# Accumulations of a seven-product block multiplication in PSUM tiles of their own, and accumulating DRAM transfers in another order and at another rate

## The chip, the cores and the metric

The kernel runs on one core of one Trainium2 chip. The metric is the device time of one execution in microseconds (us). Three runs of the kernel before gave 2103.21, 2102.78 and 2099.25 us; the median is 2102.78 us.

## The reference

Two transformer blocks follow each other on 512 tokens of width 1024, all in float32. Block 1 mixes a chunked gated delta rule (4 heads) with a differential attention (4 heads) and adds the result to its input. Block 2 puts 16 meta tokens ahead (528 tokens) and has a half-weighted feed-forward block, a hybrid mixer (retention and a sparse attention), and a second half-weighted feed-forward block. Only the feed-forward part matters here:

```python
def swiglu(u, w_gate, w_up, w_down):
    return (jax.nn.silu(u @ w_gate) * (u @ w_up)) @ w_down

h = h + 0.5 * swiglu(rmsnorm_2(h, ffn1_norm[l]), ffn1_w_gate[l], ffn1_w_up[l], ffn1_w_down[l])
h = h + hybrid_mixer(rmsnorm_2(h, mix_norm[l]), ...)
h = h + 0.5 * swiglu(rmsnorm_2(h, ffn2_norm[l]), ffn2_w_gate[l], ffn2_w_up[l], ffn2_w_down[l])
```

The feed-forward width is 2816, so that there are 22 column tiles `f` of 128 for the gate and 22 for the up weights.

## The kernel before

Activations lie transposed in SBUF (features on the 128 partitions, tokens along the free dimension). Every float32 product is made of three fp32r matmuls: a weight is split into a high part `whi` (ScalarE cast, line 238) and a rest `wlo` (VectorE subtraction, line 239), the activations likewise, and `whi*xhi + whi*xlo + wlo*xhi` is accumulated in PSUM.

One list of jobs (`jobs`) holds all weight loads of the program in the order of their use. `prefetch` issues them on SP's queue as buffers come free, `_conv` splits them (line 238 and 239, up to five split pieces ahead of the matmuls), and `w()` hands a piece to the matmuls.

**The feed-forward block (`ffn`).** The first three column tiles (`PLAIN = 3`) are multiplied plainly. The other 19 go through `pairs`, which treats gate and up weights of one `f` as a 2 x 2 block matrix (gate or up, lower or upper half of the 1024 inputs) and the tokens as two halves of 264 (256 in the second feed-forward block), and forms the four block products with seven multiplications in place of eight. Each multiplication is a `part` of 12 matmuls (4 input tiles, 3 terms each). For one `f` the parts on TensorE stand in this order, where `px`, `py` and `pz` are accumulators in PSUM:

1. `px` with the lower gate weights and the tokens `b11` (line 1053, in `begin`); ScalarE then copies it to `c1` (line 1055).
2. `py` with the token sums `t(0)` (line 1070); ScalarE then copies it to `c5` (line 1071).
3. the last part of the `f` before, into that `f`'s `px` (`end`, line 1059).
4. `px` further with `t(1)` (line 1074); ScalarE copies it to `c2` (line 1075).
5. `pz` with `b21` (line 1076); VectorE adds `c1` to it (line 1077).
6. `py` further with `b22` (line 1078); VectorE adds `c2` to it (line 1079).
7. `px` further with `t(2)` (line 1082); VectorE adds `c5` to it (line 1083).

`px` and `py` are the two halves, each one bank, of one PSUM tile `pm` of 128 x 2 x 512 (two buffers, line 1051); `pz` is a tile `sc` of its own (two buffers). The tiles `st` and `so` (one buffer of 128 x 512 each) serve the mixer. Waits between engines are put in by the tile framework, which also arranges the instructions of each engine; the first matmul of each part is kept in program order (line 1045).

`pairs` runs four times: for `f` 3 to 10 and 11 to 21 of each feed-forward block, 38 `f` in all, each time with the eight down projections of that half behind it.

**The weight sums (`sum_weights`).** Four of the seven products take sums of weight blocks. They are formed in DRAM by GpSimd's queue: plain transfers DRAM to DRAM, and transfers that accumulate (`accum_op`, line 226 to 228). The 19 column tiles are taken in ten chunks of two (the last of one). A chunk goes through six steps, eight transfers of 512 KB in all, of which each step needs the one before. The steps of different chunks are interleaved in waves: in a wave the first chunk does its step 0, the chunk before it step 1, and so on. The generator yields after each transfer and is moved on by `_conv`, once for every `bgn` splits: `bgn` is 1 for the first feed-forward block's sums (started ahead of block 1) and 3 for the second's (started ahead of the mixer). GpSimd's queue has little else: four `affine_select` of 128 x 512 (line 581) and three memsets in block 1's delta rule, four memsets in the mixer, two multiplications at the end. `pairs` reads the sums back through SP's queue as 256 KB quarters (`fraw<-wsffn`).

Of the kernel before, what the change touches and what calls it, by code (L numbers as in the profile page):

```python
# [168 lines left out]
class Net:  # L169
# [5 lines left out]
    def jobs(self, jobs):  # L175
        self.joblist = jobs
        self.j_dma = self.j_conv = self.k_conv = self.j_use = self.n_conv = self.n_use = 0
        self.p_dma = self.p_done = self.f_dma = self.f_done = 0
        self.raws, self.convd, self.wsums = {}, {}, {}
        self.bg, self.bgn = iter(()), 1  # L180
        self.kept = 0
        self.fpool = self.kslot = None
# [23 lines left out]
    def sum_weights(self, n):  # L206


        nc, a = self.nc, self.a
        nf = 22 - PLAIN  # L210
        out = self.wsums[n] = [self.dram.tile([min(2, nf - i), 4, 128, 4, 128], F32, name=f"ws{n}{i}")
                               for i in range(0, nf, 2)]
        rows = lambda x: x.rearrange("n p k c -> p n k c")

        def src(i, x):
            f = PLAIN + 2 * i
            o = 4 if x in "GU" else 0
            return a[n + ("_gate" if x in "gG" else "_up")][f:f + out[i].shape[0], :, o:o + 4, :]

        steps = (((0, "u"), (2, "g")), ((0, "U"), (2, "u")), ((1, 0),), ((1, "g"),), ((3, 1),), ((3, "G"),))  # L220
        for wave in range(len(out) + len(steps) - 1):
            for j, step in enumerate(steps):
                i = wave - j
                if 0 <= i < len(out):
                    for d, x in step:
                        y = out[i][:, x] if isinstance(x, int) else src(i, x)
                        kw = {"accum_op": OP.add} if j in (1, 3, 5) else {}
                        nc.gpsimd.dma_start(rows(out[i][:, d]), rows(y), **kw)
                        yield
# [734 lines left out]
    def ffn(self, t0, done, split=KB, half_done=None):  # L964
# [11 lines left out]
        h = n // 2  # L976
        parts = [(0, h), (h, h)] if n > 512 else [(0, n)]
        self.open_psum()
        with tc.tile_pool(name="ff", bufs=1) as pool:
# [46 lines left out]
            def gated(f, u):  # L1026
                A.copy(ahi[:, f, 0:n], u)
                V.tensor_sub(alo[:, f, 0:n], u, ahi[:, f, 0:n].bitcast(F32))

            def temp(x):  # L1030
                return pool.tile([128, n], F32, name=x, tag=x, bufs=2)
# [6 lines left out]
            def part(p, x, first=False, last=False):  # L1038

                whi, wlo = self.w()  # L1040
                for k in range(4):
                    for i, (y, z) in enumerate(((whi, 0), (whi, 1), (wlo, 0))):
                        ins = P.matmul(p, y[k], x(k)[z], start=first and k == i == 0, stop=last and k == 3 and i == 2,  # L1043
                                       skip_group_check=True)
                        if k == i == 0:
                            tc.keep_in_program_order(ins)

            def pairs(f0, f1):

                def begin():  # L1050
                    pm = self.pmain()
                    px, py = pm[:, 0, 0:h], pm[:, 1, 0:h]
                    part(px, b11, first=True)
                    c1 = pool.tile([128, h], F32, name="c1", tag="c1", bufs=2)
                    A.copy(c1, px)  # L1055
                    return px, py, c1

                def end(f, px, u, g):
                    part(px, t(3), last=True)
                    V.scalar_tensor_tensor(u[:, 0:h], px, -1.0, g[:, 0:h], op0=OP.mult, op1=OP.mult)  # L1060
                    gated(f % 11, u)

                left = None
                nxt = begin()
                for f in range(f0, f1):
                    px, py, c1 = nxt
                    pz = self.psc()[:, 0:h]
                    c2, c5 = (pool.tile([128, h], F32, name=x, tag=x, bufs=2) for x in ("c2", "c5"))
                    g, u = temp("g"), temp("u")
                    part(py, t(0), first=True)  # L1070
                    A.copy(c5, py)
                    if left:
                        end(*left)
                    part(px, t(1))
                    A.copy(c2, px)
                    part(pz, b21, first=True, last=True)
                    V.tensor_add(g[:, 0:h], pz, c1)
                    part(py, b22, last=True)
                    V.tensor_add(g[:, h:n], py, c2)
                    V.tensor_mul(g, g, r)  # L1080
                    A.activation(g, g, AF.Silu)
                    part(px, t(2))
                    V.tensor_add(u[:, h:n], px, c5)
                    V.scalar_tensor_tensor(u[:, h:n], u[:, h:n], -1.0, g[:, h:n], op0=OP.mult, op1=OP.mult)
                    left = f, px, u, g
                    if f + 1 < f1:
                        nxt = begin()
                end(*left)

            made = None  # L1090
            for half in range(2):
                for f in range(11 * half, 11 * half + 11):
                    if f >= PLAIN:
                        if f == PLAIN:
                            sides.drain(made)
                        pairs(f, 11 * half + 11)
                        break
                    hi, lo = self.w()
                    p = psum()
                    product(p, hi, lo, xs, 0, KB, True, True)  # L1100
                    if f == 0:
                        self.rstd([self.psc() for _ in range(2 if n > 512 else 1)], t0)
                        V.tensor_scalar(rh, r, 0.5, None, op0=OP.mult)
                        made = sides.add(sums())
                    g, u = temp("g"), temp("u")
                    V.tensor_mul(g, p, r)
                    A.activation(g, g, AF.Silu)
                    hi, lo = self.w()
                    p = psum()
                    product(p, hi, lo, xs, 0, KB, True, True)  # L1110
                    V.tensor_mul(u, p, g)
                    gated(f, u)
# [569 lines left out]
@with_exitstack  # L1682
def kernel(ctx: ExitStack, tc: tile.TileContext, a, out):
    net = Net(ctx, tc, a)
    net.jobs(jobs(a))
    net.setup()
    net.bg = net.sum_weights("ffn1")
    next(net.bg)
    net.block1()
    net.ffn(0, lambda m, x: net.prep(m, 2))  # L1690
    net.bg, net.bgn = net.sum_weights("ffn2"), 3
    next(net.bg)
    net.mixer()
    net.final(out)
# [17 lines left out]
```

## Time and profile before

| what | value |
|---|---|
| median of 3 runs (lowest to highest) | 2102.78 us (2099.25 to 2103.21) |
| the profiled execution: its own time | 2107.55 us |
| span of the profiled execution, first to last instruction | 2105.7 us |
| TensorE busy | 1939.5 us (92%) |
| VectorE busy, ScalarE busy | 1288.8 us (61%), 906.9 us (43%) |
| mean granted TensorE clock over the span | 0.970 of full speed |

Busy times of matmuls overlap one another and their ends are modelled, so that a share near 100% does not say that TensorE is at its peak; the starts of successive matmuls do. Idle time is put down to what released the engine. Block 1 fills about the first 460 us, the first feed-forward block lasts to about 860 us, the mixer to about 1715 us, and the second feed-forward block to the end.

### The profile page before, as it was taken

Reading aid. Unit: us, or ns where it says so; the run is one execution under the profiler, and the core shown is the slowest. Engines: PE = TensorE matmul, PEld = TensorE weight load, DVE = VectorE, ACT = ScalarE, POOL = GpSimd, SP = SyncE. Lnnn points to the kernel's source line nnn. Section 1 sums busy time; section 2 is a strip of 40 time slices with the busy share of each in tenths; the row PEclk is TensorE's granted clock in tenths of the full one; section 3 lists DMA queues with packets and bytes.
Section 4 is the critical chain, followed back from the end, with each engine's and each line's share of the span. In section 5 each row is a group of like instructions: output and inputs, shape, how many; then the busy total and the mean of one; then the engine's idle time right before and its main releaser. Section 6 shows DMA issues by size and latency. Waiting matters only on the chain. (4 is left out here: it accounts for less than half of the span.)

```text
span 2105.7 us, 31678 instructions
## 1 busy us (share of the span) xinstructions
PE 1939.5 (92%) x12138; PEld 1708.1 (81%) x12138; DVE 1288.8 (61%) x2590; ACT 906.9 (43%) x1774; POOL 153.9 (7%) x179
## 2 busy tenths in 40 slices
PE   6957668999899889999999999999999998898898
PEld 3845446888899889988989898888888888888887
DVE  4744534766655665699855454677754575646664
ACT  4523334554533553444343434344443364524553
POOL 4323443200000000000000000000000000000000
PEclk9987778999999999999999999999999999999999
DMA  9999999733434433321212121211122234434423
GB/s 296 292 231 253 264 278 257 187 131 112 152 110 120 151 117 91 120 76 66 98 68 96 66 90 61 100 61 70 61 74 97 100 129 137 148 98 150 153 87 95
DMA packets 119607, 281.36 MB, mean 134 GB/s; under 512 B 16192, under 2 KB 18720, under 8 KB 119392
## 3 DMA queue, kind: packets, MB, share of 16 engines
q1 hardware_dynamic: 86816, 198.60, 28.9%
q0 software_dynamic: 31552, 79.70, 16.2%
q8 instruction: 95, 1.56, 0.3%
q10 hardware_dynamic: 1088, 1.05, 0.1%
q14 instruction: 56, 0.46, 0.1%
HBM read 276.63 MB, written 82.36 MB: 170 GB/s over the span
## 5 line engine op out<-in xcount | busy, mean ns | idle before, releaser
L238 ACT CAST whi<-wraw 128x512 fp32r<-128x512 f32 (+1 forms) x476 | 277.1, 584 | 609.6 <-PE pm L304 473.0
L303 PE MATMUL pm<-xhi,whi 128*128 128x264 f32 (+3 forms) x1448 | 503.9, 348 | 15.4 <-DVE xc L910 14.3
L304 PE MATMUL pm<-xlo,whi 128*128 128x264 f32 (+3 forms) x1448 | 495.9, 342 | 0.0
L305 PE MATMUL pm<-xhi,wlo 128*128 128x264 f32 (+3 forms) x1448 | 494.4, 341 | 0.0
L239 DVE TENSOR_TENSOR wlo<-wraw,whi 128x512 fp32r<-128x512 f32 (+1 forms) x476 | 305.1, 641 | 206.6 <-ACT whi L238 197.6
L303 PEld LDWEIGHTS pm<-xhi,whi 128*128 128x128 f32 (+1 forms) x1448 | 276.5, 191 | 50.1 <-DVE xc L910 14.8
L305 PEld LDWEIGHTS pm<-xhi,wlo 128*128 128x128 f32 (+1 forms) x1448 | 276.0, 191 | 31.2 <-issue 2.8
L304 PEld LDWEIGHTS pm<-xlo,whi 128*128 128x128 f32 (+1 forms) x1448 | 276.4, 191 | 29.0 <-issue 2.5
L239 DVE TENSOR_TENSOR wlo<-fraw,whi 128x512 fp32r<-128x512 f32 x266 | 183.6, 690 | 127.6 <-ACT whi L238 109.3
L238 ACT CAST whi<-fraw 128x512 fp32r<-128x512 f32 x266 | 164.5, 618 | 206.8 <-issue 65.7
L1043 PE MATMUL pm<-thi,whi 128*128 128x264 f32 (+1 forms) x608 | 181.0, 298 | 56.4 <-ACT c L1055 33.9
L1043 PEld LDWEIGHTS pm<-thi,whi 128*128 128x128 f32 x608 | 115.2, 189 | 73.5 <-ACT c L1055 41.5
L1043 PE MATMUL pm<-thi,wlo 128*128 128x264 f32 (+1 forms) x608 | 172.2, 283 | 0.0
L1043 PE MATMUL pm<-tlo,whi 128*128 128x264 f32 (+1 forms) x608 | 172.1, 283 | 0.0
L303 PE MATMUL pm<-ahi,whi 128*128 128x264 f32 (+1 forms) x506 | 160.1, 316 | 0.0
L305 PE MATMUL pm<-ahi,wlo 128*128 128x264 f32 (+1 forms) x506 | 159.9, 316 | 0.0
L304 PE MATMUL pm<-alo,whi 128*128 128x264 f32 (+1 forms) x506 | 159.3, 315 | 0.0
L1043 PEld LDWEIGHTS pm<-tlo,whi 128*128 128x128 f32 x608 | 115.5, 190 | 0.0
L1043 PEld LDWEIGHTS pm<-thi,wlo 128*128 128x128 f32 x608 | 115.2, 189 | 0.0
L305 PEld LDWEIGHTS pm<-ahi,wlo 128*128 128x128 f32 x506 | 95.1, 188 | 6.1
L304 PEld LDWEIGHTS pm<-alo,whi 128*128 128x128 f32 x506 | 95.2, 188 | 5.7
L303 PEld LDWEIGHTS pm<-ahi,whi 128*128 128x128 f32 x506 | 95.2, 188 | 5.8
(456 smaller groups left out, 3532.7 us busy)
## 6 DMA issues: line engine op xcount, KB each, us to landing
wraw<-in_w_in SPq DMA_DIRECT2D x124, 512.0 KB, 3.3
fraw<-wsffn SPq DMA_DIRECT2D x152, 256.0 KB, 2.6
wsffn<-in_ffn_up POOLq DMA_DIRECT2D x54, 512.0 KB, 18.2
wsffn<-in_ffn_gate POOLq DMA_DIRECT2D x54, 512.0 KB, 17.3
fraw<-in_ffn_gate SPq DMA_DIRECT2D x76, 256.0 KB, 2.7
wsffn<-wsffn POOLq DMA_DIRECT2D x36, 512.0 KB, 17.6
wraw<-in_ffn_down SPq DMA_DIRECT2D x32, 384.0 KB, 3.0
wraw<-in_ffn_down SPq DMA_DIRECT2D x32, 320.0 KB, 2.9
```

What stands on the lines that cost most here:

```text
L238: self.nc.scalar.copy(hi, x)
L239: self.nc.vector.tensor_sub(lo, x, hi.bitcast(F32))
L303: mm(ps, whi, xhi, start=start, stop=False, **kw)
L304: mm(ps, whi, xlo, start=False, stop=False, **kw)
L305: mm(ps, wlo, xhi, start=False, stop=stop, **kw)
L1043: ins = P.matmul(p, y[k], x(k)[z], start=first and k == i == 0, stop=last and k == 3 and i == 2, skip_group_check=True)
```

## The change

Two edits. In `pairs`, `px` keeps the first half of the `pm` tile, and `py` gets a tile of its own, `st` for even and `so` for odd `f`. In `sum_weights`, the waves become groups of three chunks, each step done for the three chunks in turn; and the generator is moved on at every second split during block 1 and at every third from the first feed-forward block on.

```diff
@@ sum_weights @@
         steps = (((0, "u"), (2, "g")), ((0, "U"), (2, "u")), ((1, 0),), ((1, "g"),), ((3, 1),), ((3, "G"),))
-        for wave in range(len(out) + len(steps) - 1):
+        for i0 in range(0, len(out), 3):
             for j, step in enumerate(steps):
-                i = wave - j
-                if 0 <= i < len(out):
+                for i in range(i0, min(i0 + 3, len(out))):
                     for d, x in step:
                         y = out[i][:, x] if isinstance(x, int) else src(i, x)
                         kw = {"accum_op": OP.add} if j in (1, 3, 5) else {}
@@ pairs @@
                 def begin():
-                    pm = self.pmain()
-                    px, py = pm[:, 0, 0:h], pm[:, 1, 0:h]
+                    px = self.pmain()[:, 0, 0:h]
                     part(px, b11, first=True)
                     c1 = pool.tile([128, h], F32, name="c1", tag="c1", bufs=2)
                     A.copy(c1, px)
-                    return px, py, c1
+                    return px, c1
@@ pairs, loop over f @@
-                    px, py, c1 = nxt
+                    px, c1 = nxt
+                    py = (self.pst, self.pso)[f % 2]()[:, 0:h]
                     pz = self.psc()[:, 0:h]
@@ tile_two_blocks_kernel @@
-    net.bg = net.sum_weights("ffn1")
+    net.bg, net.bgn = net.sum_weights("ffn1"), 2
     next(net.bg)
     net.block1()
+    net.bgn = 3
     net.ffn(0, lambda m, x: net.prep(m, 2))
-    net.bg, net.bgn = net.sum_weights("ffn2"), 3
+    net.bg = net.sum_weights("ffn2")
     next(net.bg)
```

What moves on TensorE, at the first matmuls of part 2 of the second `f` of a `pairs` call (the three rows ahead are the end of part 1; `thi`, `tlo` are the token sums, and the brackets name the engine whose semaphore the row waits for). Before:

```order
L1043 MATMUL pm<-xhi,whi 128x264
L1043 MATMUL pm<-xlo,whi 128x264
L1043 MATMUL pm<-xhi,wlo 128x264
L1043 MATMUL pm<-thi,whi 128x264 [waits Activation_49]
L1043 MATMUL pm<-tlo,whi 128x264
L1043 MATMUL pm<-thi,wlo 128x264
```

With the change:

```order
L1042 MATMUL pm<-xhi,whi 128x264
L1042 MATMUL pm<-xlo,whi 128x264
L1042 MATMUL pm<-xhi,wlo 128x264
L1042 MATMUL st<-thi,whi 128x264
L1042 MATMUL st<-tlo,whi 128x264
L1042 MATMUL st<-thi,wlo 128x264 [waits DVE_49]
```

The wait for ScalarE at the first matmul of part 2 is gone; a wait for VectorE stands at the third, the first that needs the converted `wlo` piece. The parts themselves follow each other as before.

The same at the first matmul of part 7 of that `f` (ahead of it the end of part 6). Before:

```order
L1043 MATMUL pm<-xlo,whi 128x264
L1043 MATMUL pm<-xhi,wlo 128x264
L1043 MATMUL pm<-thi,whi 128x264 [waits DVE_49]
L1043 MATMUL pm<-tlo,whi 128x264
L1043 MATMUL pm<-thi,wlo 128x264
```

With the change:

```order
L1042 MATMUL st<-xlo,whi 128x264
L1042 MATMUL st<-xhi,wlo 128x264
L1042 MATMUL pm<-thi,whi 128x264 [waits Activation_49]
L1042 MATMUL pm<-tlo,whi 128x264
L1042 MATMUL pm<-thi,wlo 128x264 [waits DVE_49]
```

The first matmul waited for VectorE, which reads `py`; it now waits for ScalarE's copy `c2` of `px`, two parts back.

On GpSimd's queue, chunks of the first feed-forward block in block 1 (`wsffn` with a number is a chunk; the brackets name the transfer queue's semaphores, eight used in turn, whose earlier transfer the row waits for). Before:

```order
L228 DMA wsffn_100<-in_ffn_up 128x2x512 [waits DMASW0_49]
L228 DMA wsffn_100<-in_ffn_gate 128x2x512 [waits DMASW1_49]
L228 DMA wsffn_99<-in_ffn_up 128x2x512 [waits DMASW2_49]
L228 DMA wsffn_99<-in_ffn_up 128x2x512 [waits DMASW3_49]
L228 DMA wsffn_98<-wsffn_98 128x2x512 [waits DMASW4_49]
L228 DMA wsffn_97<-in_ffn_gate 128x2x512 [waits DMASW5_49]
L228 DMA wsffn_96<-wsffn_96 128x2x512 [waits DMASW6_49]
L228 DMA wsffn_95<-in_ffn_gate 128x2x512 [waits DMASW7_49]
```

With the change:

```order
L227 DMA wsffn_97<-in_ffn_gate 128x2x512 [waits DMASW7_49,DMASW4_49]
L227 DMA wsffn_98<-in_ffn_gate 128x2x512 [waits DMASW5_49]
L227 DMA wsffn_99<-in_ffn_gate 128x2x512 [waits DMASW6_49,DMASW1_49]
L227 DMA wsffn_97<-wsffn_97 128x2x512 [waits DMASW7_49]
L227 DMA wsffn_98<-wsffn_98 128x2x512 [waits DMASW3_49,DMASW0_49]
L227 DMA wsffn_99<-wsffn_99 128x2x512 [waits DMASW1_49]
L227 DMA wsffn_97<-in_ffn_gate 128x2x512 [waits DMASW2_49]
L227 DMA wsffn_98<-in_ffn_gate 128x2x512 [waits DMASW3_49]
L227 DMA wsffn_99<-in_ffn_gate 128x2x512 [waits DMASW4_49]
```

Before, each row waits for the transfer eight places back. With the change these rows wait for the one three places back; of the 24 transfers of a group nine do so, the other fifteen wait for one four to six places back or for none. In both programs 51 transfers stand ahead of the first `affine_select`, 4 between it and the second, and all 160 (the second feed-forward block's too) ahead of the mixer's memsets. SP's queue has the same order in both, and TensorE, ScalarE and VectorE have the same order in block 1.

## Rows read from the trace of the kernel before

**Rows 1.** The page: TensorE's busy time, then tenths in 40 slices.

```profile
PE 1939.5 (92%) x12138; PEld 1708.1 (81%) x12138; DVE 1288.8 (61%) x2590; ACT 906.9 (43%) x1774; POOL 153.9 (7%) x179
...
PE   6957668999899889999999999999999998898898
...
PEclk9987778999999999999999999999999999999999
DMA  9999999733434433321212121211122234434423
```

**Rows 2.** Stretches: us; engines' busy us (instructions); clock, DMA share, GB/s.

```profile
200.00:250.00 50.00, 31.30 (x117) 22.84 (x117) 20.02 (x77) 14.04 (x30) 21.16 (x24) 0.67 1.05 259
550.00:600.00 50.00, 45.68 (x362) 44.17 (x362) 32.95 (x59) 24.88 (x49) 0.00 (x0) 1.00 0.49 147
600.00:650.00 50.00, 50.00 (x415) 50.00 (x414) 20.69 (x39) 12.64 (x26) 0.00 (x0) 1.00 0.31 89
```

**Rows 3.** TensorE's waits in the pairs: us in total, times, longest us.

```profile
PE pm L1043 <- ACT c L1055: 33.9, 37, 1.2
...
PE pm L1043 <- DVE g L1079: 17.7, 34, 0.5
...
PE pm L1043 <- ACT c L1071: 3.5, 4, 0.9
```

**Rows 4.** Timeline of TensorE, first feed-forward block: start us, us, instruction, [idle before <-releaser].

```profile
500.30 0.28 PE L1043 MATMUL pm<-xhi,wlo 128*128 128x264 f32 x1
501.49 0.39 PE L1043 MATMUL pm<-thi,whi 128*128 128x264 f32 x1 [0.91 <-ACT c L1055]
501.72 0.28 PE L1043 MATMUL pm<-tlo,whi 128*128 128x264 f32 x1
...
505.68 0.29 PE L1043 MATMUL sc<-xhi,whi 128*128 128x264 f32 x1
...
507.13 0.28 PE L1043 MATMUL pm<-xhi,whi 128*128 128x264 f32 x1
...
508.46 0.28 PE L1043 MATMUL pm<-xhi,wlo 128*128 128x264 f32 x1
509.27 0.39 PE L1043 MATMUL pm<-thi,whi 128*128 128x264 f32 x1 [0.53 <-DVE g L1079]
```

**Rows 5.** Timeline of TensorE, second feed-forward block.

```profile
1753.62 0.28 PE L1043 MATMUL pm<-xhi,wlo 128*128 128x256 f32 x1
1754.42 0.39 PE L1043 MATMUL pm<-thi,whi 128*128 128x256 f32 x1 [0.52 <-DVE g L1079]
...
1757.28 0.28 PE L1043 MATMUL pm<-xhi,wlo 128*128 128x256 f32 x1
1758.46 0.39 PE L1043 MATMUL pm<-thi,whi 128*128 128x256 f32 x1 [0.91 <-ACT c L1055]
```

**Rows 6.** Timeline of GpSimd: the sums ahead of the first affine_select.

```profile
1.27 0.89 POOL L228 DMA_DIRECT2D wsffn<-in_ffn_up  x1 [0.82 <-POOLq L1703]
...
118.31 1.16 POOL L228 DMA_DIRECT2D wsffn<-in_ffn_up  x1 [3.71 <-DMA wsffn<-in_ffn_up]
129.80 0.64 POOL L581 TENSOR_SCALAR_AFFINE_SELECT te<-te 128x512 f32<-128x512 f32 x1 [10.32 <-DVE te L580]
```

**Rows 7.** Line 228 (the sums), whole run: durations ns, first and last start; landing.

```profile
L228 POOL DMA_DIRECT2D wsffn<-in_ffn_gate x60: 562/1128/1643, 2.1 to 403.2; - x60
...
DMA to landing us min/median/max: 4.5/17.7/32.4
```

**Rows 8.** DMA, first 400 us: queue, packets, MB, share; weight loads' us to landing.

```profile
q0 software_dynamic: 31084, 78.68, 83.7%
...
wraw<-in_w_in SPq DMA_DIRECT2D x32, 512.0 KB, 8.4
```

**Rows 9.** DMA in the mixer, 900 to 1100 us: the same loads.

```profile
wraw<-in_w_in SPq DMA_DIRECT2D x23, 512.0 KB, 3.2
```

**Rows 10.** Waits in the first 400 us: ScalarE's split for the weight loads.

```profile
ACT whi L238 <- DMA wraw<-in_w_in: 77.2, 10, 27.3
```

## The prediction

> **What bounds the kernel now.** I read the page first, then the stretches of 50 us, then TensorE's own waits and its timeline, and last the transfers and GpSimd. On the page [rows 1] TensorE is busy for 92% of the span and ten tenths full almost everywhere outside two places: the first seven slices (block 1), where its clock is also granted at less than full speed and the DMA engines are full, and the stretches at 8 tenths around slices 10 to 16 and 34 to 39, which are the `pairs` of the two feed-forward blocks. The stretches [rows 2] tell the two places apart. From 200 to 250 us (block 1) TensorE is busy for 31 of 50 us at a mean clock of 0.67, and the DMA share is 1.05. From 550 to 600 us (`pairs`) it runs at full clock, has 45.7 us busy with 362 matmuls, and the transfers take half of the DMA engines; in the down projections from 600 to 650 us, where nothing is waited for, it starts 415 matmuls of the same width. So the pairs lose time at full clock and the cause is not the DMA.
>
> TensorE's waits [rows 3] name it: 33.9 us for ScalarE's copy `c1`, 17.7 us for VectorE's sum at line 1079 and 3.5 us for the copy `c5`. The timeline [rows 4] shows where. Within a stream, a part of 12 matmuls takes 505.68 to 507.13, 1.45 us, so 0.121 us from start to start. At the start of part 2 the next matmul comes 1.19 us after the last of part 1 (500.30 to 501.49), and the one behind it 0.23 us later; at part 7 it comes 0.81 us after part 6 (508.46 to 509.27). Part 2 writes `py` and the copy it waits for reads `px`; part 7 writes `px` and the sum it waits for reads `py`. They share nothing but the tile.
>
> **Part one, `py` in its own tile.** As the order shows, both waits lose their engine. What stands in their place is older: part 2 now needs only the `st` or `so` buffer of two `f` ago, and part 7 the copy `c2`, which ScalarE starts two parts (2.9 us) earlier. So I take the whole gap. In the first feed-forward block the stall at part 2 costs 1.19 - 0.12 + 0.23 - 0.12 = 1.18 us, that at part 7 0.81 - 0.12 + 0.11 = 0.80 us. The first `f` of each of the four calls has no part 3 between, so that part 4 waits for `c5` as part 2 for `c1`: four stalls in [rows 3], with the same 1.18 us. The last `f` of a call has no stall at part 7 (34 waits, not 38), since matmuls of the down projection stand there. For 19 `f` that makes 19 x 1.18 + 17 x 0.80 + 2 x 1.18 = 38.4 us. In the second feed-forward block [rows 5] the gaps are 1758.46 - 1757.28 = 1.18 and 1754.42 - 1753.62 = 0.80 us against 0.12, with the same 0.11 us for the late second matmul: 1.17 and 0.79 us, and 19 x 1.17 + 17 x 0.79 + 2 x 1.17 = 38.0 us. Together **76.4 us**. The other end is the idle time as the profile counts it [rows 3], 33.9 + 17.7 + 3.5 = 55.1 us, which lets a matmul's modelled tail of 0.28 us count as work; as the tail overlaps the next matmul everywhere else, I stay at 76.4.
>
> What is late next? An `f` shrinks from 84 x 0.121 + 1.98 = 12.1 to 10.2 us. VectorE is busy for 32.95 of 50 us there [rows 2], 8.0 us per `f`, and ScalarE for 24.88, 6.0 us; both fit, VectorE with 2.2 us to spare, and up to five split pieces lie ahead of the matmuls. The wait for VectorE that now stands at the third matmul of part 2 is for such a piece, four parts old. The transfers rise from 0.49 to 0.49 x 12.1 / 10.2 = 0.58 of the DMA engines. So nothing gives the gap back, as long as no sums run beside the pairs.
>
> **Part two, the sums.** The diff changes a rate in the program, but no rate in time: GpSimd's queue has nothing that ties a transfer to a split. In both programs 51 transfers stand ahead of the first `affine_select`, and all 160 are ahead of the mixer. In the trace all of them start between 1.3 and 403 us [rows 6, 7], the second feed-forward block's too, and take 83.7% of the DMA engines over 400 us [rows 8]. So they spread no further than before, and the load on block 1 stays. What does change is how many are under way: eight before, now three to six. The first 51 started within 1.27 to 118.31 us [rows 6], 2.34 us each; a median landing of 17.7 us [rows 7] over eight is 2.2 us, so that the DMA engines' throughput sets the pace and the landing is mostly queueing. Three under way would then land in about 7 us and keep the same pace, if a lone transfer is faster than that; the shortest in the trace is 4.5 us [rows 7], for one of the 256 KB ones, and a 512 KB one should add half of 2.2 us: 5.6 us, below 7.
>
> What it does to block 1 no row shows, so I bound it. The splits wait there 77.2 us for weight loads [rows 10], which land in 8.4 us against 3.2 us in the mixer, where no sums run [rows 8, 9]. Were the load's delay to fall with the number of sums queued, from eight to about five, the 77 us would give 77.2 x (8.4 - 3.2) / 8.4 x 3/8 = 18 us. Were the sums a tenth slower, the first `affine_select`, for which GpSimd now arrives 10.3 us early [rows 6], would be reached 11.7 us later: a loss of about 2 us there and perhaps 10 us with the three behind it. Between -18 and +10 I take 0, since the trace says that the DMA engines stay full. Behind the sentence on the loads stands a rule of the Trainium skill (DMA: Bandwidth & Descriptors, section Queues, rings and completion order): each engine goes round robin between the queues that have work, so that what counts is whether the sums' queue is empty, not how long it is. By it the term is 0 as well, and the 18 us are not to be had; by the reading above they are.
>
> **The sum.** 2107.55 - 76.4 + 0 = 2031.2 us for the profiled execution. Its time stands 4.8 us above the median of the runs, so the median should be 2102.8 - 76.4 = **2026.4 us**.
>
> **The rivals.**
> 1. *Block 1 is relieved* after all, because the sums' queue runs dry with three under way or during the waits at the four `affine_select`. For it: those waits hold GpSimd 10 us at a time, longer than three transfers last (7 us). Against: the DMA share of 1.05. Up to 77.2 x (8.4 - 3.2) / 8.4 = 48 us if the queue were always dry; two thirds of that give 2026.4 - 32 = 1994 us.
> 2. *The split pieces become the bound of the pairs.* VectorE's and ScalarE's order is fixed, and a conversion behind a VectorE sum that waits for TensorE may come late. For it: only 2.2 us of slack per `f`. Against: ScalarE has 4 us of slack, and a piece is split several parts ahead of its use. If half of the gain is lost: 2026.4 + 38 = 2064 us.
> 3. *Slower: the sums are bound by their landing.* If three under way still land in 17.7 us, they go at 5.9 us each; at five to six under way 3.2 us. Of the first 51, 18 are of the first kind: 18 x 5.9 + 33 x 3.2 = 212 us, and the first `affine_select` is reached 82 us after VectorE's operand (129.8 us). All of the delta rule stands behind it: 2026.4 + 82 = 2108 us. It decides from the point where the landing is above 129.8 / (18/3 + 33/5.5) = 10.8 us; below that no `affine_select` is late. Against it is the 7 us above. Of this the Trainium skill says (the same page, section Anatomy of one DMA, SWDGE path) that such a transfer costs a fixed 2 us and its bytes over 436 GB/s; my estimate from that is 3.2 us for 512 KB and 1.1 us each with three under way, by which rival 3 is out and the sum stays. The trace has 2.34 us each, so the page's rate is not reached here.
>
> **How the numbers follow.** Forecast 74%, rival 1 13%, rival 2 7%, rival 3 6%. The forecast's own range is 2026.4 - 18 to 2026.4 + 10 with the full gap, and 2026.4 + 21 = 2047 where only the counted idle time goes; rival 1 reaches below it, rivals 2 and 3 above. For 8 in 10 I take 2005 to 2047: it leaves out most of rivals 1, 2 and 3. A measurement of this kernel tells 0.2% (4 us) from no change. Forecast and rivals 1 and 2 are faster by more: 94%; of rival 3 I give 1% to no change and 5% to slower.
>
> **What would show it.** Right: TensorE's waits no longer list line 1043 behind the copies or the sum; an `f` in the pairs takes 10.2 us, and a stretch of 50 us there holds some 410 matmuls, as the down projections do; the last sum still starts between 390 and 440 us and the first `affine_select` near 130 us. Wrong: new waits of line 1043 for the split pieces (rival 2); a first `affine_select` after 140 us with a wait for a sum in front of it (rival 3); a DMA share well below 1 in the first 350 us and fewer waits for `wraw` (rival 1). Sums that last beyond 480 us would also show in the pairs, as waits of the splits for `fraw`.

## The result, and the profile after

The changed kernel takes 2014.72 us (median of 4 runs, 2012.99 to 2016.05) against 2102.78 us: a ratio of 0.9584, 95% interval 0.9568 to 0.9601. The prediction was 2026.4 us; the time is inside its range and 11.7 us below its value. The profiled execution took 2014.84 us, its span is 2013.0 us.

Where the time went is read from the last rows of each stage. The additions to `hT` close block 1 (eight on line 943), the first feed-forward block (eight on line 1123 between 700 and 900 us) and the mixer (line 1594). Before (count, durations in ns, first to last start in us):

```profile
L943 DVE TENSOR_TENSOR hT<-pm,hT x8: 691/692/693, 422.6 to 460.7; 128x512 f32<-128x512 f32 x8
L1123 DVE TENSOR_TENSOR hT<-hT,u x8: 699/701/702, 804.6 to 861.0; 128x528 f32<-128x528 f32 x8
L1594 DVE TENSOR_TENSOR hT<-pm,hT x8: 690/692/693, 1671.5 to 1709.6; 128x512 f32<-128x512 f32 x8
```

After, the same three (the program's lines are one lower):

```profile
L942 DVE TENSOR_TENSOR hT<-pm,hT x8: 682/692/693, 406.0 to 444.1; 128x512 f32<-128x512 f32 x8
L1122 DVE TENSOR_TENSOR hT<-hT,u x8: 700/702/702, 749.5 to 805.9; 128x528 f32<-128x528 f32 x8
L1593 DVE TENSOR_TENSOR hT<-pm,hT x8: 690/692/693, 1617.1 to 1655.2; 128x512 f32<-128x512 f32 x8
```

The stages take, before and after: block 1 460.7 and 444.1 us (-16.6), the first feed-forward block 400.3 and 361.8 (-38.5), the mixer 848.6 and 849.3, the second feed-forward block 396.1 and 357.8 us (-38.3, by the spans). So the two blocks with `pairs` gave 76.8 us and block 1 the rest.

The page of after, TensorE's rows and the slices [rows 1]:

```profile
PE 1920.7 (95%) x12138; PEld 1705.7 (85%) x12138; DVE 1284.2 (64%) x2590; ACT 904.4 (45%) x1774; POOL 153.6 (8%) x179
...
PE   6957878999999999999999999999999999999998
...
PEclk8978878999999999999999999999999999999999
DMA  9999999994534533321222221211122234535532
```

The tenths of 8 in the feed-forward blocks are gone but for the last slice; block 1 still has its first seven slices, and the DMA engines are now full for nine slices, not seven. The stretches of after [rows 2]:

```profile
200.00:250.00 50.00, 41.63 (x187) 31.13 (x188) 34.65 (x128) 22.80 (x58) 20.61 (x25) 0.86 1.01 258
...
500.00:550.00 50.00, 50.00 (x416) 50.00 (x415) 39.21 (x70) 31.37 (x60) 0.00 (x0) 1.00 0.58 182
```

In the `pairs` TensorE starts 416 matmuls in 50 us, as in the down projections before. TensorE's waits over the whole run [rows 3] begin with block 1's alone, and line 1042 (1043 before) is not among them:

```profile
PE pf L819 <- DVE dfk L791: 16.1, 4, 7.7
PE pm L302 <- DVE xc L909: 10.9, 1, 10.9
PE pd L302 <- ACT xhi L356: 10.7, 5, 7.5
```

TensorE's timeline [rows 4] has the two places: part 1 to part 2 of one `f`, part 6 to part 7 of it, and part 1 to part 2 of the next:

```profile
492.38 0.28 PE L1042 MATMUL pm<-xhi,wlo 128*128 128x264 f32 x1
492.51 0.28 PE L1042 MATMUL st<-thi,whi 128*128 128x264 f32 x1
...
499.65 0.29 PE L1042 MATMUL st<-xhi,wlo 128*128 128x264 f32 x1
499.77 0.29 PE L1042 MATMUL pm<-thi,whi 128*128 128x264 f32 x1
...
502.55 0.28 PE L1042 MATMUL pm<-xhi,wlo 128*128 128x264 f32 x1
502.67 0.28 PE L1042 MATMUL so<-thi,whi 128*128 128x264 f32 x1
```

Both gaps are now 0.12 to 0.13 us, the spacing of the stream, and an `f` takes 502.67 - 492.51 = 10.16 us.

In block 1 the sums last longer than before. Their line [rows 7], with the last start at 457.4 us, and their landing:

```profile
L227 POOL DMA_DIRECT2D wsffn<-in_ffn_gate x60: 692/1146/2074, 2.2 to 457.4; - x60
...
DMA to landing us min/median/max: 3.0/11.8/28.6
```

GpSimd's timeline [rows 6] at the first and the fourth `affine_select`:

```profile
136.54 1.16 POOL L227 DMA_DIRECT2D wsffn<-in_ffn_up  x1
137.24 1.15 POOL L227 DMA_DIRECT2D wsffn<-in_ffn_gate  x1
137.94 1.13 POOL L227 DMA_DIRECT2D wsffn<-in_ffn_up  x1
138.72 1.09 POOL L580 TENSOR_SCALAR_AFFINE_SELECT te<-te 128x512 f32<-128x512 f32 x1
...
192.11 0.69 POOL L227 DMA_DIRECT2D wsffn<-wsffn  x1 [10.90 <-DMA wsffn<-in_ffn_up]
197.62 1.16 POOL L227 DMA_DIRECT2D wsffn<-in_ffn_gate  x1 [4.82 <-DMA wsffn<-wsffn]
198.35 1.09 POOL L580 TENSOR_SCALAR_AFFINE_SELECT te<-te 128x512 f32<-128x512 f32 x1
```

VectorE's operands for these two were written from 132.91 to 133.60 and from 188.18 to 188.87 us, so that the selects start 5.1 and 9.5 us late, behind sums that wait for sums. Before, GpSimd was early [rows 6]. ScalarE, which needs the selects, waits 4.5 us for them (us in total, times, longest; first 400 us):

```profile
ACT te L582 <- POOL te L580: 4.5, 1, 4.5
```

And yet block 1 is shorter. SP's timeline shows from where on: the delta rule sends a matrix to DRAM (`db`, four transfers of 64 KB) and reads it back. Before:

```profile
190.81 7.06 SPq L611 DMA_DIRECT2D db<-slot  x4
217.27 0.45 SPq L613 DMA_DIRECT2D slot<-db  x1
```

After:

```profile
202.02 6.63 SPq L610 DMA_DIRECT2D db<-slot  x4
214.39 0.45 SPq L612 DMA_DIRECT2D slot<-db  x1
```

The write starts 11.2 us later, but from write to read back it is 12.4 us in place of 26.5. Late selects are not all of the 11.2 us: the write of `rd`, ahead of the first of them, already starts at 111.18 us in place of 103.97. At the read back after is 2.9 us ahead; the other 13.7 of block 1's 16.6 us come behind it, where VectorE and ScalarE wait less for the small transfers that follow (`krow` and `dx`). Their waits in the first 400 us, before:

```profile
DVE dfk L792 <- DMA krow<-rdfd: 27.9, 4, 9.6
...
ACT slot L645 <- DMA slot<-dx: 20.2, 3, 11.0
```

After, with ScalarE's wait for the weight loads [rows 10] ahead of them:

```profile
ACT whi L237 <- DMA wraw<-in_w_in: 72.3, 9, 27.8
...
DVE dfk L791 <- DMA krow<-rdfd: 16.5, 4, 8.9
...
ACT slot L644 <- DMA slot<-dx: 7.3, 1, 7.3
```

The granted TensorE clock is no rival for this gain: its mean over block 1 is 0.87 before and 0.88 after. My estimate of what it costs there, TensorE's busy time times the missing share of the clock, summed over stretches of 50 us, is 39.5 us before and 39.9 after.

The DMA answers over the first 400 us [rows 8] say the same: the sums' queue has 79.3% against 83.7%, the weight loads land in 7.5 against 8.4 us, and `db` in half the time. Before:

```profile
db<-slot SPq DMA_DIRECT2D x4, 64.0 KB, 19.8
```

After:

```profile
q0 software_dynamic: 28562, 72.46, 79.3%
...
wraw<-in_w_in SPq DMA_DIRECT2D x32, 512.0 KB, 7.5
...
db<-slot SPq DMA_DIRECT2D x4, 64.0 KB, 9.9
```

### The profile page after: what moved, and what is told of

It is laid out like the page before. It is cut to its first block, busy times and chain, and to the rows that moved or that the text cites. A ratio compares the mean times of both kernels' runs of the same rounds, so it can differ in the third digit from the quotient of the medians.

```text
span 2013.0 us, 31731 instructions
## 1 busy us (share of the span) xinstructions
PE 1920.7 (95%) x12138; PEld 1705.7 (85%) x12138; DVE 1284.2 (64%) x2590; ACT 904.4 (45%) x1774; POOL 153.6 (8%) x179
## 3 DMA queue, kind: packets, MB, share of 16 engines
q0 software_dynamic: 31552, 79.70, 17.4%
## 4 chain that ended last, share of the span: by engine, by line
PE 82%; DMA 12%; DVE 3%; issue 2%; POOL 0%; ACT 0%; SPq 0%; DVEq 0%; POOLq 0%; ACTq 0%
PE pm L302 18%; PE pm L304 18%; PE pm L303 18%; PE pm L1042 11%; DMA wsffn<-in_ffn_up 4%; PE so L1042 3%; PE sc L1042 3%; PE st L1042 3%; DMA wsffn<-wsffn 2%; DMA wsffn<-in_ffn_gate 2%; PE sc L302 2%; PE sc L303 1%; PE sc L304 1%; DMA krow<-rdfd 1%; DVE rot L1208 1%
## 5 line engine op out<-in xcount | busy, mean ns | idle before, releaser
L304 PEld LDWEIGHTS pm<-xhi,wlo 128*128 128x128 f32 (+1 forms) x1448 | 276.1, 191 | 31.3 <-issue 2.7
L1042 PE MATMUL pm<-thi,whi 128*128 128x264 f32 (+1 forms) x456 | 129.7, 284 | 0.0
L1042 PE MATMUL pm<-thi,wlo 128*128 128x264 f32 (+1 forms) x456 | 129.1, 283 | 0.0
L1042 PE MATMUL pm<-tlo,whi 128*128 128x264 f32 (+1 forms) x456 | 129.0, 283 | 0.0
L1042 PEld LDWEIGHTS pm<-thi,whi 128*128 128x128 f32 x456 | 86.6, 190 | 0.9 <-DVE u L1082 0.9
L1042 PEld LDWEIGHTS pm<-tlo,whi 128*128 128x128 f32 x456 | 86.7, 190 | 0.0
## 6 DMA issues: line engine op xcount, KB each, us to landing
wsffn<-in_ffn_gate POOLq DMA_DIRECT2D x54, 512.0 KB, 10.8
```

The lines of the kernel that those rows point to most:

```text
L304: mm(ps, wlo, xhi, start=False, stop=stop, **kw)
```

## The experiments

The theory after the result: the tile of its own gives the pairs' 77 us; the groups of three do two opposite things in block 1, they shorten the way of its small transfers (fewer sums under way) and delay the `affine_select` (more sums that wait in front of it). Rivals: the pairs' gain hides something else; block 1's gain is scatter, or comes from the grouping and not from the number under way. Stages below are from the traces, in us; the `db` column has the start of the write and the time to the read back. A ratio is to runs of before taken beside that kernel; their medians were 2102.78 to 2109.72 us, so medians of different rows compare to some us only. The stages are of one execution each, which lies up to 8.4 us from its kernel's median.

| kernel | median us | ratio to before (95%) | `db` at, way | block 1 | feed-forward 1 | mixer | feed-forward 2 |
|---|---|---|---|---|---|---|---|
| before | 2102.78 | | 190.8, 26.5 | 460.7 | 400.3 | 848.6 | 396.1 |
| after | 2014.72 | 0.9584 (0.9568 to 0.9601) | 202.0, 12.4 | 444.1 | 361.8 | 849.3 | 357.8 |
| psum_only | 2037.15 | 0.9667 (0.9642 to 0.9693) | 191.6, 26.7 | 458.4 | 361.8 | 848.8 | 357.9 |
| order_only | 2094.57 | 0.9934 (0.9916 to 0.9951) | 204.4, 12.3 | 447.1 | 400.4 | 848.6 | 396.7 |
| group1 | 2029.89 | 0.9628 (0.9602 to 0.9653) | 218.4, 8.9 | 460.4 | 361.9 | 849.3 | 358.3 |
| group10 | 2027.9 | 0.9628 (0.9609 to 0.9648) | 192.4, 26.3 | 456.3 | 361.9 | 849.1 | 358.4 |
| after_dve | 1991.23 | 0.9461 (0.9429 to 0.9493) | 184.3, 17.4 | 414.1 | 362.0 | 848.8 | 358.5 |
| group1_dve | 1996.57 | 0.9487 (0.9468 to 0.9505) | 181.4, 11.8 | 417.0 | 369.5 | 848.8 | 358.4 |
| defer | 2015.8 | 0.9574 (0.9557 to 0.959) | 206.7, 11.7 | 416.8 | 361.9 | 876.1 | 357.9 |
| anchored13 | 1950.66 | 0.9276 (0.9237 to 0.9316) | 158.2, 9.1 | 366.6 | 361.4 | 858.5 | 358.0 |
| anchored13_dve | 1946.1 | 0.9239 (0.9214 to 0.9265) | 158.3, 7.4 | 371.7 | 361.4 | 859.3 | 358.0 |
| anchored13_waves | 1945.76 | 0.9251 (0.9214 to 0.9289) | 152.9, 16.5 | 366.3 | 361.4 | 855.3 | 357.7 |
| anchored23 | 1926.95 | 0.915 (0.9121 to 0.918) | 142.2, 6.5 | 346.2 | 362.8 | 859.2 | 357.7 |
| spread_only | 2000.25 | 0.9491 (0.9467 to 0.9515) | 139.2, 6.4 | 340.6 | 400.0 | 858.9 | 395.6 |

**psum_only**: the new tile for `py`, the sums as before.

```diff
-                    pm = self.pmain()
-                    px, py = pm[:, 0, 0:h], pm[:, 1, 0:h]
+                    px = self.pmain()[:, 0, 0:h]
...
+                    py = (self.pst, self.pso)[f % 2]()[:, 0:h]
```

> The sums are those of before (waves, rates 1 and 3); only py has its own PSUM tile. Theory A: the new tiles give 76 us in the pairs and nothing else, and what the change gained beyond that (12 us of the median, 16.6 us of block 1 in the profiled executions) comes from the order of the sums. Then block 1 ends as before (last line that adds its output at 460 us, within 4 us), an f of the pairs takes 10.2 us, and the median is 2102.8 - 76.4 = 2026 us (2022 to 2031). Rival B: the order of the sums does nothing, and block 1 is shorter for another reason (the program's other waits, or chance); then block 1 ends near 444 us and the median is 2015 us.

Both feed-forward blocks have the whole gain, and block 1 stays within 2.3 us, as theory A says. The median misses A's 2022 to 2031 us by 6 us: the runs scatter over 18 us (2028.73 to 2047.15), with a mean granted clock of 0.971 in the fastest, which is the profiled one, and 0.961 in the slowest.

**order_only**: the groups of three, with the rates 1 and 3 of before and `px` and `py` in one tile as before.

```diff
-        for wave in range(len(out) + len(steps) - 1):
+        for i0 in range(0, len(out), 3):
...
-                i = wave - j
-                if 0 <= i < len(out):
+                for i in range(i0, min(i0 + 3, len(out))):
```

> Only the order of the sums is changed (groups of three), with the rates 1 and 3 of before; px and py share a tile as before. Theory A: block 1 ends near 444 us instead of 461 us, the pairs stay at 12.1 us for an f, and the median is 2103 - 12 = 2091 us (2086 to 2096). Rival B: no change, 2103 us.

The feed-forward blocks stay as they were, and block 1 gives 13.6 us: 0.5 to 0.8% by the ratio, small but clear of no change. As in after, the write of `db` starts late and its way is halved. The waits are shared out differently, though: ScalarE waits 26.7 us for the selects (4.5 in after) and 57.2 us for weight loads (72.3). The two ratios multiply to 0.9603, just above the interval of after (to 0.9601) and well within the scatter of psum_only: the parts act apart. The rate of the change was not run alone; order_only has most of the gain without it.

**group1** and **group10**: after, with groups of one and with one group of ten (there with the rate 1 in block 1).

```diff
-        for i0 in range(0, len(out), 3):
+        for i0 in range(0, len(out), 1):
...
-                for i in range(i0, min(i0 + 3, len(out))):
+                for i in range(i0, min(i0 + 1, len(out))):
```

> As the changed kernel, with groups of one chunk in place of three, so that one or two sums are under way at a time. If the number under way is what matters (theory A1), the sums' queue runs emptier: their share of the DMA engines in the first 400 us falls from 79% to about 55% (a lone transfer lands in 4.5 to 6 us, so 160 of them, mostly one or two at a time, take 500 to 650 us), weight loads in block 1 land in 5 to 6 us, block 1 ends at 425 to 440 us, but the last sums run beside the first feed-forward block's pairs and cost 5 to 20 us there: 2005 to 2025 us. If instead it is a matter of which transfers stand next to each other (A2), block 1 ends at 444 us or later. If the first affine_select comes much later than 139 us for want of faster sums (the prediction's third rival), block 1 ends after 460 us.

> As the changed kernel, with one group of all ten chunks (and the rate 1 in block 1, which alone leaves the order on GpSimd's queue as it is), so that eight sums are under way at a time, as with the waves of before. A1 (the number under way matters): block 1 ends near 460 us as before and the median is 2026 us, as with the PSUM tiles alone. A2 (the grouping itself matters): near 2015 us.

group10 is as A1 says (456.3 us, 2027.9 us): eight under way by groups cost what eight by waves did, so it is not the grouping. group1 misses A1: block 1 ends at 460.4 us, the median is 2029.89 us, the sums' queue has 77.3% in place of about 55%, and the weight loads land in 7.8 us in place of 5 to 6. It is the third case named there, the late select: the first starts at 159.1 us. With one chunk at a time the way of `db` is shortest of the three and its start latest, with ten it is as before in both, and both kernels are slower than after. SP's timeline of group1:

```profile
218.35 2.81 SPq L610 DMA_DIRECT2D db<-slot  x4
227.28 0.45 SPq L612 DMA_DIRECT2D slot<-db  x1
```

Its waits from 100 to 215 us give the reason of the late start, ScalarE behind all four selects:

```profile
ACT te L582 <- POOL te L580: 41.7, 4, 20.6
```

**after_dve** and **group1_dve**: after and group1, with the four selects and three memsets of block 1 taken from GpSimd. In the select's place stand a clamp at zero ahead of the exponential and a multiplication by the triangular mask behind it, both on VectorE.

```diff
-                    G.affine_select(out=p4(E), in_=p4(E), pattern=[[0, 4], [1, 128]], compare_op=OP.is_ge,
-                                    fill=NEG, base=0, channel_multiplier=-1)
+                    V.tensor_scalar(E, E, 0.0, None, op0=OP.min)
                     A.activation(E, E, AF.Exp)
+                    V.tensor_tensor(p4(E), p4(E), self.triu[:, None, :].to_broadcast([128, 4, 128]), op=OP.mult)
```

> As the changed kernel, but the delta rule's four affine_select and three memsets leave GpSimd's queue: VectorE takes the minimum with 0 ahead of the exponential, multiplies by the triangle behind it, and does the memsets (some 8 us more of VectorE in block 1). Theory T: the order of the sums does two things to block 1. Fewer under way lets its own transfers land sooner (the four 64 KB transfers of db and of dx in 10 us, from 20 us), and sums in front of the affine_select make these late (by 9, 7, 12 and 19 us against before); the first is worth some 30 us, the second costs some 15 us. Then this kernel's block 1 ends at 425 to 435 us and the median is 2000 to 2006 us. Rival R: the late affine_select cost nothing, since the path leads through the loads: then no change, 2015 us, or some 5 us more for VectorE's added work.

> The same edit on the kernel with groups of one chunk, in which the affine_select came 29, 16, 33 and 32 us late and block 1 ended at 460 us. T: block 1's transfers keep their short landings (slot<-rd 12.5 us, db 6 us) and nothing is late any more, so that block 1 ends at 420 to 432 us and the median is 1990 to 2003 us. R: block 1 ends near 455 us, 2025 us.

Off the sums' queue, the delta rule has no sums in front of it: 30.0 us off block 1 in after, 43.4 in group1, 23 and 33 us by the medians. R is out. T priced it too low: after_dve gains 11 us more in block 1 and 9 us more by the median than its bounds, group1_dve 3 us more in block 1. How much is the selects' lateness alone is not isolated. The write of `db` starts 17.8 us earlier than in after, but its way is 17.4 us in place of 12.4 with the same groups of three, and its landing 15.2 us where T said 10; and the mean granted clock over block 1 rises from 0.88 to 0.93, worth 17 us by the estimate above (39.9 to 22.8). group1_dve loses 7.6 us in the first feed-forward block. Its sums last to 478 us, but those of after_dve last to 461 us, 47 us into that block, and cost it 0.2 us; in group1_dve the clock also falls, to 0.68 from 430 to 440 us. Which of the two it was is open.

**defer**: the second feed-forward block's sums held back until behind the mixer's four memsets, one per two splits there.

```diff
+                        if n == "ffn2":
+                            self.tc.keep_in_program_order(ins)
```

> As the changed kernel, but the second feed-forward block's sums are pinned on GpSimd's queue behind the mixer's memsets, so that only 80 of the 160 transfers stand in block 1. T: up to the affine_select nothing changes (138 to 198 us); from about 230 us on no sum runs beside block 1, its remaining loads land in 3.3 us, and it ends at 425 to 438 us: 1996 to 2008 us, if the sums in the mixer (at 870 to 1080 us, where the DMA share is 0.2 to 0.3) cost nothing there, as a weight load of 512 KB is needed only every 5.7 us. If block 1 does not depend on the DMA engines in its second half (R), 2015 us.

Block 1 gains 27.3 us, 8 us more than T's bounds allow, and the mixer loses 26.8: the sums run there in one heap. So the median is R's number, but not for R's reason. The stretch of it (columns as in [rows 2]):

```profile
850.00:950.00 100.00, 94.22 (x533) 79.11 (x531) 82.86 (x193) 41.80 (x79) 30.46 (x32) 0.98 1.01 254
```

So it is not enough to move the load; a heap costs elsewhere too.

**anchored13**: each sum is held behind a copy of one element, on GpSimd, of the piece that was just split, so that the program's rate becomes a rate in time: one sum per split in block 1, one per three later. Copies and sums are kept in program order.

```diff
+        ins = self.nc.gpsimd.tensor_copy(self.mark, lo[0:1, 0, 0:1].bitcast(F32))
+        self.tc.keep_in_program_order(ins)
...
+                        ins = nc.gpsimd.dma_start(rows(out[i][:, d]), rows(y), **kw)
+                        self.tc.keep_in_program_order(ins)
...
+            self.anchor(lo)
```

> Each sum is tied to a split in time: GpSimd copies one element of the piece just split and the transfer is pinned behind that copy; one for each split in block 1, one for every third from the first feed-forward block on. So all 80 of the first block's sums run in block 1, spread over it, and the second's in the mixer. T: half of the sums' load on block 1 is gone, few are under way at a time, and block 1 ends at 410 to 430 us: 1983 to 2003 us. Against it: copies that wait for a split now stand ahead of the affine_select on GpSimd's queue and could make them late, then no better than 2015 us.

Block 1 ends at 366.6 us and the median is 1950.66 us: the direction of T, and more than twice its gain, for it left 43 us of block 1 and 32 us of the median unforeseen. No run tells why in full; block 1's mean granted clock is 0.96 here (0.88 in after), 29 us by the estimate above.

**anchored13_dve**, **anchored13_waves**, **anchored23**: the same with the selects on VectorE, with the order of before, and with one sum per two splits in block 1, which are the rates of the change. The line of the last, against anchored13:

```diff
-    net.bg, net.bgn = net.sum_weights("ffn1"), 1
+    net.bg, net.bgn = net.sum_weights("ffn1"), 2
```

> The sums tied in time (one per split in block 1, one per three splits later) and, besides, the four affine_select and the three memsets of block 1 moved from GpSimd to VectorE. Theory (two effects in block 1 that act apart: the depth and the number of sums under way, and the sums that stand ahead of the affine_select on GpSimd's queue): with the sums tied in time few stand ahead, the first affine_select already starts at 105 us, so moving them is worth much less than the 23 us it was worth with the untied sums: 0 to 12 us, 1939 to 1951 us. Rival (the queue costs the same 23 us however many sums are in front): about 1928 us. Rival on the other side (GpSimd's select was hidden, and VectorE now has the work on the path): 1951 to 1958 us.

> The sums tied in time as in the fastest kernel so far, but in the order of before (waves) in place of the groups of three. Theory (what helps is how many sums are under way at a time; with the sums tied to the splits, the order no longer sets that): the same as with the groups, 1946 to 1958 us, block 1 within 6 us of 366.6. Rival (the order of three matters by itself): block 1 10 us or more longer, 1960 us or more.

> The changed kernel with its rates made true in time: each sum is held behind a one-element GpSimd copy of the piece that was just split, one sum per two splits in block 1 and one per three from the first feed-forward block on. Theory (block 1's loss is the sums' load, and the pairs have transfers to spare: 0.58 of the engines): block 1 ends earlier still than with one per split (366.6 us), by up to 15 us, and the pairs lose less than that as long as the sums arrive ahead of their use: 1935 to 1955 us. Rival (the sums of the first feed-forward block come too late for the pairs that read them): the pairs of the first feed-forward block take 20 us or more above 361 us, and the whole is at 1960 us or more.

With the sums tied in time, block 1 is 77.5 us shorter than in after, and with the change's own rates 98 us. All three are of the theory's side: anchored13_dve lies within its bounds, anchored13_waves 0.2 us below them, and anchored23 gains more than the theory gave it (20 us off block 1 for 15, 1927 us for 1935 at the least), with the pairs 1.4 us longer. The order (waves or threes) then does nothing to block 1 (366.3 and 366.6 us), though the way of `db` is 16.5 us with waves and 9.1 with threes. The selects may as well stay on GpSimd: block 1 is 5 us longer with them on VectorE, but that execution lies 6 us above its kernel's median, and the medians can't tell the two apart. anchored23 is the fastest kernel of the study, faster than before and after. SP's timeline of it at `db`:

```profile
142.16 0.34 SPq L617 DMA_DIRECT2D db<-slot  x1
...
143.71 1.72 SPq L617 DMA_DIRECT2D db<-slot  x3
148.66 0.45 SPq L619 DMA_DIRECT2D slot<-db  x1
```

Its first 400 us of DMA, beside those of after above:

```profile
q0 software_dynamic: 10244, 26.14, 30.1%
...
wraw<-in_w_in SPq DMA_DIRECT2D x32, 512.0 KB, 3.7
...
db<-slot SPq DMA_DIRECT2D x4, 64.0 KB, 3.0
```

Its stretches in block 1 and in the first pairs:

```profile
200.00:250.00 50.00, 49.41 (x504) 39.33 (x503) 31.94 (x101) 34.25 (x81) 3.71 (x8) 1.00 0.34 104
400.00:450.00 50.00, 49.06 (x405) 48.72 (x404) 36.92 (x67) 29.32 (x56) 12.79 (x22) 1.00 0.99 283
```

The pairs bear a nearly full load of the DMA engines (0.99) with 405 matmuls started, where 416 is the stream's own rate, and the whole stage is 1.0 us longer than in after; block 1 does not bear it. ScalarE's waits for weight loads in the first 400 us fall to 14.5 us, from 72.3 in after and 77.2 before [rows 10]:

```profile
ACT whi L238 <- DMA wraw<-in_w_in: 14.5, 8, 4.9
```

**spread_only**: anchored23 with `px` and `py` in one tile again.

```diff
-                    px = self.pmain()[:, 0, 0:h]
+                    pm = self.pmain()
+                    px, py = pm[:, 0, 0:h], pm[:, 1, 0:h]
...
-                    py = (self.pst, self.pso)[f % 2]()[:, 0:h]
```

> The sums tied in time at the change's own rates (one per two splits in block 1, one per three later), but py back in the second half of the px tile as before. Theory (the two parts of the change act in different stages and add): block 1 as in the kernel with both (346 us within 6), the pairs' stages back at about 400 and 396 us, so 1927 + 77 = 2004 us, 1998 to 2010. Rival (with sums beside the pairs, the DMA engines, full from 400 to 450 us there, are what limits the first pairs, and the stalls in PSUM hide in that): the first feed-forward block gains less than 30 us from the separate tiles, and the whole is at 1995 us or less.

Theory holds, the rival is out: 2000.25 us, block 1 within 5.6 us, the feed-forward blocks back at 400.0 and 395.6 us, and TensorE's two waits too [rows 3]:

```profile
PE pm L1049 <- ACT c L1061: 33.6, 37, 0.9
PE pm L1049 <- DVE g L1085: 17.7, 34, 0.5
```

The separate tile is worth 73.3 us by the medians and 75.1 us by the two stages even with sums beside the pairs.

## Why the prediction was right, and where it was off

- **Both waits in the pairs go, 76.4 us.** Right to half a microsecond: 38.4 and 38.0 were forecast for the two blocks, 38.5 and 38.3 measured, and psum_only and spread_only show it with and without the other part. The spacing of the starts was the right measure and not the counted idle time, 55.1 us. `f` was put at 10.2 us (10.16), the stretch at some 410 matmuls (416), the DMA share at 0.58 (0.58).
- **Nothing gives it back in the pairs.** Right: VectorE is busy for 39.2 of 50 us, no wait of a matmul of line 1042 appears, and rival 2 is out.
- **A rate in the program, none in time.** Right: all sums still lie in the first 457 us. anchored23 shows what those rates would be worth if they held: 88 us below after.
- **"Three under way would then land in about 7 us and keep the same pace".** Wrong. The median landing is 11.8 us, the last sum starts at 457.4 us (390 to 440 were named), and the first select at 138.7 us (near 130). Rival 3's price point, a landing above 10.8 us, was a good one: the landing is just above it and the selects are late by 5.1 and 9.5 us. Its mechanism is there; its size, 82 us, is not.
- **"Between -18 and +10 I take 0, since the trace says that the DMA engines stay full".** This is the step that was off: block 1 gave 16.6 us, 13.6 with the order alone, close to the -18 end. It is nearly the whole distance between 2031.2 and 2014.84 us of the profiled executions. The share of the sums' queue (83.7 and 79.3%) did not say how long a small transfer waits among them. The -18 was also looked for at the wrong transfers: the waits for weight loads changed little (77.2 to 72.3 us), and they do not go with block 1 (57.2 us in order_only, and 53.0 in group1, whose block 1 is no shorter than before), while the way of `db` fell by 14.1 us and the waits for `krow` and `dx` by 11.4 and 12.9. A rule of the Trainium skill stood behind the 0 (DMA: Bandwidth & Descriptors, section Queues, rings and completion order: each engine goes round robin between the queues that have work). By it a shorter queue of sums that is never empty would leave `db` as it was. The runs have 64 KB landing in 19.8 us before, 9.9 in after and 3.0 in anchored23. While `db` is on its way, the sums' queue moves 2089 packets before (in 26.5 us, 91.2% of the engines) and 967 after (in 12.4 us, 82.2%), beside nearly as many on SP's queue (2475 and 2386). Were turns taken and the sums' queue never empty, the same `db` should let about as many packets of the sums pass both times; it let half as many pass. So the measurement does not speak against the rule: by these counts it is "never empty" that failed, which the prediction took from the share. This is read from the counts, and not isolated.
- **Rival 1** had the direction of it, and far too small a price for the whole load: its upper bound of 48 us counted the weight loads alone. With the sums spread out (26.1 of 78.7 MB in the first 400 us) block 1 is 114.5 us shorter (460.7 to 346.2). Some 35 us of that go with the granted clock (0.87 and 0.99 over block 1; 39.5 and 4.6 us by the estimate above); whether the clock rose because TensorE waited less, no run isolates.

So the gain of the order part is the difference of two effects, rivals 1 and 3 in part, that mostly cancel. That they did, and so left the total inside the range, is in part luck: the reasoning for the 0 was another. The halved way of `db` is not block 1's gain by itself: it makes up for the late start and 2.9 us more, and the rest comes with `krow` and `dx` behind it. This is read from the timelines, not isolated. Open as well is the mixer's 10 us with tied sums beside it; TensorE's waits there name none above 2.4 us.

## What to carry to other kernels

Two accumulators that are halves of one tile wait for each other's readers; where a wait names a reader of the other half, give each a tile, and price it by the spacing of the starts. A rate at which a program issues transfers is only a rate in time if something in the queue waits for the work that it should follow; otherwise all of them go at once, ahead of whatever stands behind them. And where transfers fill the engines, look at the round trips of the small transfers on the critical path, and not at the share alone.

## What the runs showed of the hardware that was not expected

- The four 64 KB transfers of `db` on SP's queue landed sooner with fewer sums under way, at an almost equal share of the sums' queue: 19.8 us with eight and 9.9 us with three to six, at 83.7% and 79.3%. It is no fixed price, and not one of all small transfers: after_dve has 15.2 us with the same groups, and from before to after the 128 KB of `krow` went from 7.9 to 6.1 us and the 32 KB of `rd` from 5.9 to 6.4.
- Three to six transfers of 512 KB under way were not as fast as eight: the first 51 sums started within 137.9 us in place of 118.3, 2.7 us each against 2.34.
- At full clock and with its operands prefetched, TensorE lost little beside full DMA engines: 405 matmuls in 50 us at a share of 0.99, against 416 at 0.58. In block 1 the granted clock was higher where TensorE was busier: from 200 to 250 us 0.67 before (31.3 us busy), 0.86 after (41.6 us busy), 1.00 in anchored23 (49.4 us busy), the first two being means between its two levels.
